# A four-layer hybrid decoder on one core: VectorE's running sums, modulated rows and rsqrt operands moved to PSUM, and the first layer's modulation computed two feature tiles at a time

## The chip, the cores and the metric

One core of one Trainium2 chip. The metric is device time in microseconds (us) of one execution of the whole program, the median of several runs.

## The reference

Four layers over 512 tokens of 1024 features, batch 1, all in float32. Layer i has mixer i mod 3: 0 is multi-head latent attention (MLA, 8 heads), 1 is sliding-window attention with sinks (SWA, 16 heads, window 128), 2 is native sparse attention (NSA). So layers 0 and 3 are MLA.

```python
cond = jax.nn.silu(c)
for i in range(DEPTH):
    shift, scale, gate = jnp.split(cond @ ada_w[i] + ada_b[i], 3, axis=-1)
    h = rmsnorm(x, norm_g[i]) * (1 + scale[:, None, :]) + shift[:, None, :]
    ...                      # x = x + gate * Mixer(h); mixer = (attention * silu(gate path)) @ w_out
# MLA: q_a, kv_a, k_pe, gate = split(h @ w_in, 256 | 128 | 64 | 1024)
#      q = rmsnorm(q_a) @ w_q_b ; kv = rmsnorm(kv_a) @ w_kv_b ; rope on k_pe and part of q
```

`ada_w[i]` is 1024 x 3072, so the modulation of a layer reads 12.6 MB. A third of it (shift, scale or gate) is 1024 x 1024.

## The kernel before, in words

Every float32 product on TensorE (PE) is made of three products of rounded parts: `mm3` issues hi*hi, hi*lo and lo*hi (lines 70, 71, 72). A weight piece of 512 columns comes by DMA from SyncE's queue (SP), ScalarE (ACT) rounds it to `wh` (line 103) and GpSimd (POOL) subtracts to get `wl` (line 104). VectorE (DVE) does the same subtraction for activations (line 66), evicts PSUM, and forms the softmax and the rotations.

The order of instructions on each engine is written by a planner at compile time: it takes the program's order as priority, and simulates when buffers come free. On the chip each engine then runs its list strictly in order.

**Modulation of layers 1 to 3 and the gate of layer 0.** `ada_steps` works on one third at a time: 16 loads of 128 x 512 of `ada_w` into three buffers; for each, VectorE multiplies by a column of `cond` and adds into `ada_acc`, a tile in SBUF (lines 315 and 317). For the thirds queued with a third argument True ((0, 2), (1, 0) and (3, 2)) the later half of the rows is multiplied by ScalarE (line 311) and added by GpSimd (line 313). At the end TensorE sums over the partitions (`rows` at line 323 or `cols` at line 329). There are ten such thirds. `queue_mods` puts the steps into a queue, and `mod_steps` takes them out at fixed places of the attention heads and of the output projection.

**First layer.** `start` loads the four token tiles of x (SP), squares them on ScalarE, makes the reciprocal root on VectorE (`rsqrt`, lines 78 to 83) and scales x on VectorE (line 1162). Then for each feature tile k of 8, `prep(k)` loads 1 MB of `ada_w` (two loads of 512 KB in runs of 128 floats), sums it over the 8 rows in `facc` (SBUF, lines 1179 and 1181; for k = 0 on TensorE, line 1186), sums over the partitions (line 1189), adds the bias (line 277), transposes x (line 151), modulates (line 1197) and splits into `hTh`, `hTl`. The products of tile k (four tiles of 448 columns and a gate tile of 512, 15 matmuls) follow. `angles()`, the rotation's sine and cosine, is called at k = 6.

**Norm of the later layers.** `norm_tile` transposes a normalised token tile into two PSUM banks of pool `tpp`. In each half ScalarE modulates two of the four feature tiles and VectorE two (lines 384, 386), into `hf` in SBUF; then the split (lines 387, 388).

**MLA's low-rank part.** The four token tiles of 448 columns are copied to `lat` in SBUF (lines 611, 613), squared on ScalarE, `rsqrt` runs on 128 x 8 tiles in SBUF (lines 85 to 87), `lat` is scaled (lines 625, 626) and transposed (line 151), and only then come the head projections. The rotation of the key part reads `lat` (lines 158, 161).

**PSUM.** Eight banks: projections `mmp`, transposes `tpp`, scores `sp`, outputs `op`: 2, 2, 2, 2 in layer 0 and 2, 3, 2, 1 in layers 1 to 3. Every softmax block is transposed through a `tpp` bank and split from there by ScalarE (line 65) and VectorE (line 66). The gate tiles of MLA take a bank of `op`.

## Time and profile before

| what | value |
|---|---|
| median of 3 runs | 1137.04 us (1131.63 to 1139.35) |
| span of the profiled execution | 1138.5 us |
| TensorE matmul busy | 1041.8 us, 92% of the span |
| VectorE / GpSimd / ScalarE busy | 836.5 / 651.8 / 634.3 us |
| HBM read and written | 124.17 MB and 8.39 MB |

The profiled execution has no time of its own beside its span; the span lies within the three runs, 1.5 us above their median, so what lies around the span is no more than the runs differ among themselves. An engine's busy time is time in which one of its instructions runs or is held, so a VectorE instruction that waits for something in the middle of its execution counts as busy and merely looks long. "Granted clock" is TensorE's: 1.00 is 2.4 GHz, 0.5 is 1.2 GHz, and a stretch between them is a mixture.

### The profile page before, as it was taken

The page shows a single profiled execution, that of the slowest core. Times are in us where ns is not written, and L with a number is a line of the kernel's source. Part 1 is how long each engine was busy: PE and PEld are TensorE (multiplying, and loading weights), DVE is VectorE, ACT ScalarE, POOL GpSimd, SP SyncE. Part 2 cuts the span into 40 slices and gives each one's busy share as a digit, 9 for nine tenths or more (in the row PEclk, how much of TensorE's full clock was granted, in tenths as well). Part 3 has the DMA queues.
Part 4 walks back from the last instruction along what each step waited for, and adds up shares of the span by engine and source line. Part 5 has one row for each costly group of instructions (what it writes and reads, how often), then busy time and mean ns, then how long its engine had stood idle before and what let it go on. Part 6 is the DMA issues. An engine that isn't in the chain of part 4 may idle for free.

```text
span 1138.5 us, 21101 instructions
## 1 busy us (share of the span) xinstructions
PE 1041.8 (92%) x6836; PEld 939.1 (82%) x6836; DVE 836.5 (73%) x2361; ACT 634.3 (56%) x1622; POOL 651.8 (57%) x781
## 2 busy tenths in 40 slices
PE   5798999989998998999899999999998896999997
PEld 4586888889887887999878798988888895889897
DVE  6967576588899787783748887789996687657435
ACT  3455666444545686356344567768784265656542
POOL 2564755292766784914665756757565627534473
PEclk9889999998989998999999899999999898999999
DMA  9935442374573212743662611211006526211141
GB/s 291 239 85 152 135 132 79 112 242 151 151 229 93 74 39 94 230 147 84 187 171 73 169 27 32 56 38 38 10 30 221 178 102 199 61 55 49 39 139 74
DMA packets 146026, 133.93 MB, mean 118 GB/s; under 512 B 31462, under 2 KB 118652, under 8 KB 145916
## 3 DMA queue, kind: packets, MB, share of 16 engines
q1 hardware_dynamic: 142688, 122.55, 37.0%
q10 hardware_dynamic: 3228, 10.04, 2.5%
q8 instruction: 54, 0.88, 0.3%
q14 instruction: 56, 0.46, 0.1%
HBM read 124.17 MB, written 8.39 MB: 116 GB/s over the span
## 4 chain that ended last, share of the span: by engine, by line
PE 60%; DVE 17%; DMA 8%; issue 6%; ACT 5%; POOL 4%; SPq 1%; DVEq 0%; ACTq 0%; POOLq 0%
PE mm L70 8%; PE mm L71 8%; PE mm L72 8%; PE tp L151 7%; DMA ada_w<-ada_w 6%; DVE ada_acc L317 4%; PE o L70 4%; PE o L71 3%; PE o L72 3%; DVE facc L1181 2%; PE mm L416 2%; PE s L966 1%; PE s L965 1%; PE o L974 1%; PE o L975 1%
## 5 line engine op out<-in xcount | busy, mean ns | idle before, releaser
L104 POOL TENSOR_TENSOR wl<-raw,wh 128x512 fp32r<-128x512 f32 (+2 forms) x206 | 274.9, 1346 | 127.7 <-ACT wh L103 103.6
L103 ACT ACTIVATE wh<-raw 128x512 fp32r<-128x512 f32 (+2 forms) x206 | 124.5, 612 | 113.8 <-PE o L71 27.8
L70 PE MATMUL mm<-wh,hTh 128*128 128x256 f32 (+2 forms) x512 | 153.7, 301 | 7.9 <-DVE sg L428 3.4
L71 PE MATMUL mm<-wl,hTh 128*128 128x256 f32 (+2 forms) x512 | 152.7, 298 | 0.0
L72 PE MATMUL mm<-wh,hTl 128*128 128x256 f32 (+2 forms) x512 | 152.4, 298 | 0.2 <-DVE hTl L388 0.2
L530 ACT ACTIVATE p<-p,negm 128x128 f32<-128x128 f32 (+3 forms) x192 | 107.0, 558 | 46.6 <-DVE negm L526 43.6
L70 PEld LDWEIGHTS mm<-wh,hTh 128*128 128x128 f32 x512 | 100.4, 196 | 10.9 <-DVE sg L428 3.9
L533 POOL TENSOR_SCALAR p<-p,rsum,bg 128x128 f32<-128x128 f32 (+3 forms) x128 | 82.0, 647 | 45.4 <-DVE rsum L532 36.3
L526 DVE CUSTOM_DVE_ANT_0 p<-s,mask 128x128 f32<-128x128 f32 (+3 forms) x192 | 91.0, 483 | 22.0 <-PE s L966 9.0
L71 PEld LDWEIGHTS mm<-wl,hTh 128*128 128x128 f32 x512 | 100.5, 196 | 1.6
L72 PEld LDWEIGHTS mm<-wh,hTl 128*128 128x128 f32 x512 | 100.4, 196 | 1.6 <-DVE hTl L388 0.4
L151 PE MATMUL tp<-ident,p 128*128 128x128 f32 x480 | 79.4, 274 | 1.9 <-POOL p L533 0.9
L533 POOL TENSOR_SCALAR p<-p,rsum 128x128 f32<-128x128 f32 (+1 forms) x64 | 34.7, 546 | 78.2 <-DVE rsum L532 71.2
L66 DVE TENSOR_TENSOR ptl<-tp,pth 128x512 fp32r<-128x512 f32 x108 | 72.2, 683 | 9.7 <-ACT pth L65 9.0
L481 POOL TENSOR_TENSOR x<-x,res 128x256 f32<-128x256 f32 x48 | 42.4, 888 | 60.8 <-DVE res L480 40.3
L65 ACT ACTIVATE pth<-tp 128x512 fp32r<-128x512 f32 x108 | 60.9, 591 | 26.1 <-PE tp L151 22.9
L151 PEld LDWEIGHTS tp<-ident,p 128*128 128x128 f32 x480 | 58.0, 140 | 12.2 <-POOL p L533 1.9
L355 ACT ACTIVATE sq_junk<-x 128x256 f32<-128x256 f32 x64 | 26.5, 414 | 67.5 <-POOL x L481 57.6
L317 DVE SCALAR_TENSOR_TENSOR ada_acc<-ada_w,res,ada_acc 128x512 f32<-128x512 f32 x42 | 52.3, 1265 | 11.0 <-DMA ada_w<-ada_w 10.7
L70 PE MATMUL mm<-wh,ogh 128*128 128x256 f32 x192 | 55.1, 288 | 3.3 <-DVE res L480 1.7
L72 PE MATMUL mm<-wh,ogl 128*128 128x256 f32 x192 | 53.9, 285 | 1.0 <-DVE ogl L66 0.8
L71 PE MATMUL mm<-wl,ogh 128*128 128x256 f32 x192 | 54.1, 282 | 0.0
(380 smaller groups left out, 3556.6 us busy)
## 6 DMA issues: line engine op xcount, KB each, us to landing
ada_w<-ada_w SPq DMA_DIRECT2D x160, 256.0 KB, 3.2
raw<-swa_w_in SPq DMA_DIRECT2D x36, 256.0 KB, 3.3
raw<-nsa_w_in SPq DMA_DIRECT2D x36, 256.0 KB, 3.1
aw<-ada_w SPq DMA_DIRECT2D x16, 512.0 KB, 7.1
raw<-mla_w_in SPq DMA_DIRECT2D x32, 256.0 KB, 3.1
raw<-mla_w_out SPq DMA_DIRECT2D x32, 256.0 KB, 2.8
xd<-x SPq DMA_DIRECT2D x12, 512.0 KB, 3.2
x<-xd ACTq DMA_DIRECT2D x12, 512.0 KB, 6.6
```

The lines of the kernel that those rows point to most:

```text
L65: self.nc.scalar.activation(hi, src, AF.Copy)
L66: self.nc.vector.tensor_sub(lo, src, hi.bitcast(F32))
L70: mm(out, ah, bh, start=start, stop=False, skip_group_check=True)
L71: mm(out, ah, bl, start=False, stop=False, skip_group_check=True)
L72: mm(out, al, bh, start=False, stop=stop, skip_group_check=True)
L103: nc.scalar.activation(wh, raw, AF.Copy)
L104: nc.gpsimd.tensor_sub(wl, raw, wh.bitcast(F32))
L151: self.nc.tensor.transpose(out, in_, self.ident[:k, :k])
L317: nc.vector.scalar_tensor_tensor(a, w, self.condl[:, k:k + 1], a, op0=OP.mult, op1=OP.add)
L526: nc.vector.tensor_tensor_reduce(p[:, :L], s, mask, -scale, init, op0=OP.add, op1=OP.min, accum_out=nm)
L530: nc.scalar.activation(p[:, :W], p[:, :W], AF.Exp, bias=nm, scale=-1.0, accum_out=sm)
L533: nc.gpsimd.tensor_scalar(p[:, :L], p[:, :L], r, 0.5 if gate is None else gate, op0=OP.mult, op1=OP.mult)
```

## The change

Six edits in one.

1. **Sums in PSUM.** Pool `accp` with one PSUM bank exists in layers 0, 1 and 3. `ada_steps` sums one half of 512 columns at a time in that bank (during the output projection, in a bank of `sp`), and the last of the eight adds writes SBUF. In NSA (layer 2) there is no such bank and the sum stays in SBUF. The ScalarE and GpSimd share of three thirds goes: every add is VectorE's. In the queue the closing step of a third now comes ahead of the next third's loads.
2. **Banks.** 2, 2, 2, 1, 1 in layers 0, 1 and 3: one output bank fewer in layer 0, one transpose bank fewer in layers 1 and 3. NSA keeps 2, 3, 2, 1.
3. **Modulated rows in PSUM.** `norm_tile` modulates in place in the transposes' bank, the first half all on ScalarE, the second half all on VectorE, and splits from there.
4. **MLA.** `rsqrt` has its input and its scratch in PSUM. The key part is rotated straight from the projection's bank, in the loop that copies the low-rank part.
5. **First layer.** Four groups of two feature tiles: eight loads of 256 KB in runs of 256 floats into twelve buffers, sums of 128 x 512 in PSUM, all on VectorE; no modulation on TensorE. x's reciprocal root has its six small steps on GpSimd, and x is scaled on ScalarE. The sine and cosine come before the sums. One of the four 448-column products takes a transpose bank.
6. `rsqrt` of one column uses `tensor_scalar` with two pointer scalars in place of `scalar_tensor_tensor`.

```diff
-BANKS = ((2, 3, 2, 1), (2, 3, 2, 1), (2, 3, 2, 1))
+BANKS = ((2, 2, 2, 1, 1), (2, 2, 2, 1, 1), (2, 3, 2, 1, 0))
-    def rsqrt(self, half, n, y):
+    def rsqrt(self, half, n, y, t=None, eng=None):
+        if n == 1:
+            t = self.small.tile([P, n], F32, name="rs_t", tag="rs_t")
+        eng = eng or nc.vector
         nc.vector.tensor_scalar(y.bitcast(I32), half.bitcast(I32), -0.5, 1593268703.0 - 2.0 ** 31, op0=OP.mult, op1=OP.add)
-        t = self.small.tile([P, n], F32, name="rs_t", tag=f"rs_t{n}")
         for _ in range(3):
             if n == 1:
-                nc.vector.scalar_tensor_tensor(t, y, half, y, op0=OP.mult, op1=OP.mult)
-                nc.vector.tensor_scalar(y, t, -1.5, y, op0=OP.add, op1=OP.mult)
+                eng.tensor_scalar(t, y, half, y, op0=OP.mult, op1=OP.mult)
+                eng.tensor_scalar(y, t, -1.5, y, op0=OP.add, op1=OP.mult)
             else:
-                nc.vector.tensor_mul(t, y, y)
-                nc.vector.tensor_mul(t, t, half)
+                nc.vector.tensor_mul(t, half, y)
+                nc.vector.tensor_mul(t, t, y)
...
+    def acc_bank(self):
+        if self.in_proj_out:
+            return self.sp.tile([P, 512], F32, name="s")
+        return self.accp and self.accp.tile([P, 512], F32, name="acc")
...
-                n = 4 if self.acc_bufs > 1 else 0
-                self.mods += loads[:n] + late + loads[n:]
+                self.mods += late + loads
...
-                for c in range(0, D, 512):
-                    a = acc[0][:, c:c + 512]
+                c = 512 * (step // 4)
+                if step % 4 == 0:
+                    acc[1:] = [self.acc_bank() or acc[0][:, c:c + 512]]
+                for k in (2 * (step % 4), 2 * (step % 4) + 1):
                     w = self.adaw.tile([P, 512], F32, name="ada_w", tag="ada_w", bufs=3)
                     nc.sync.dma_start(w, dr(A["ada_w"], l * D * 3 * D + k * 3 * D + third * D + c, [[KT * 3 * D, P], [1, 512]]))
-                    if pool and k > 3:
-                        d = w if k else a
-                        nc.scalar.activation(d, w, AF.Copy, scale=self.condl[:, k:k + 1])
-                        if k:
-                            nc.gpsimd.tensor_add(a, a, w)
-                    elif k == 0:
-                        nc.vector.tensor_scalar(a, w, self.condl[:, 0:1], None, op0=OP.mult)
+                    if k == 0:
+                        nc.vector.tensor_scalar(acc[1], w, self.condl[:, 0:1], None, op0=OP.mult)
                     else:
-                        nc.vector.scalar_tensor_tensor(a, w, self.condl[:, k:k + 1], a, op0=OP.mult, op1=OP.add)
+                        d = acc[0][:, c:c + 512] if k == KT - 1 else acc[1]
+                        nc.vector.scalar_tensor_tensor(d, w, self.condl[:, k:k + 1], acc[1], op0=OP.mult, op1=OP.add)
...
-                if kk in ACT_K:
-                    nc.scalar.activation(hf[:, kk, :], ps[:, k * P:(k + 1) * P], AF.Identity, scale=s, bias=b)
+                h = ps[:, k * P:(k + 1) * P]
+                if half == 0:
+                    nc.scalar.activation(h, h, AF.Identity, scale=s, bias=b)
                 else:
-                    nc.vector.tensor_scalar(hf[:, kk, :], ps[:, k * P:(k + 1) * P], s, b, op0=OP.mult, op1=OP.add)
-            nc.scalar.activation(self.nhTh[:, ks, t], hf[:, ks], AF.Copy)
-            nc.vector.tensor_sub(self.nhTl[:, ks, t], hf[:, ks], self.nhTh[:, ks, t].bitcast(F32))
+                    nc.vector.tensor_scalar(h, h, s, b, op0=OP.mult, op1=OP.add)
+            hf = ps.rearrange("p (k q) -> p k q", q=P)
+            self.split_dve(self.nhTh[:, ks, t], self.nhTl[:, ks, t], hf)
...                                                      # mla: low-rank part
+                k1 = ap.tile([P, 1, 2, 64], F32, name="kpe", tag="kpe", bufs=4)
+                self.rope_twice(ps[:, None, 384:448], 1, i, k1)
...
+            ps = self.sp.tile([P, 512], F32, name="s")
+            nc.vector.tensor_scalar(ps[:, 0:4], ss[:, 0:4], 0.5 / 256, 0.5 * EPS, op0=OP.mult, op1=OP.add)
+            nc.vector.tensor_scalar(ps[:, 4:8], ss[:, 4:8], 0.5 / 128, 0.5 * EPS, op0=OP.mult, op1=OP.add)
-            self.rsqrt(ss, 8, rs)
+            self.rsqrt(ps[:, 0:8], 8, rs, ps[:, 8:16])
...                                                      # start
+            for i, x in enumerate(xs):
+                nc.scalar.activation(junk, x, AF.Square, accum_out=ss[:, i:i + 1])
+            self.angles(pf, fr)
+            for i, x in enumerate(xs):
+                h = ss[:, i:i + 1]
+                nc.vector.tensor_scalar(h, h, 0.5 / D, 0.5 * EPS, op0=OP.mult, op1=OP.add)
+                self.rsqrt(h, 1, rstds[i], eng=nc.gpsimd)
+            for i, x in enumerate(xs):
+                nc.scalar.activation(x, x, AF.Copy, scale=rstds[i])
+            ps4 = [p.tile([P, 512], F32, name=n) for p, n in ((self.sp, "s"), (self.sp, "s"), (self.op, "o"), (self.tpp, "tp"))]
...
+            def columns(g):
+                pool, name = ((self.mmp, "mm"), (self.accp, "acc"))[g % 2]
+                a = pool.tile([P, 512], F32, name=name).rearrange("p (t n) -> p t n", t=2)
+                acc = ap.tile([P, 2, 256], F32, name="facc", tag="facc", bufs=2)
+                for r in range(KT):
+                    w = ap.tile([P, 2, 256], F32, name="aw", tag="aw", bufs=12)
+                    nc.sync.dma_start(w, dr(A["ada_w"], r * 3 * D + g * 256, [[KT * 3 * D, P], [D, 2], [1, 256]]))
+                    if r == 0:
+                        nc.vector.tensor_scalar(a, w, self.cond[:, 0:1], None, op0=OP.mult)
+                    else:
+                        nc.vector.scalar_tensor_tensor(acc if r == KT - 1 else a, w, self.cond[:, r:r + 1], a, op0=OP.mult, op1=OP.add)
+                weights(2 * g)
+                weights(2 * g + 1)
+                return acc
...
+            acc = columns(0)
+            self.vector_columns(vs)
+            modulation(0, acc)
+            features(0)
+            for k in range(KT):
+                g = k // 2 + 1
+                if k % 2 == 0 and g < 4:
+                    acc = columns(g)
+                elif g < 4:
+                    modulation(g, acc)
+                if k + 1 < KT:
+                    features(k + 1)
+                products(k)
```

## Rows read from the trace of the kernel before

**Rows 1.** The page: busy time by engine, and the chain that ended last by engine.
```profile
PE 1041.8 (92%) x6836; PEld 939.1 (82%) x6836; DVE 836.5 (73%) x2361; ACT 634.3 (56%) x1622; POOL 651.8 (57%) x781
...
PE 60%; DVE 17%; DMA 8%; issue 6%; ACT 5%; POOL 4%; SPq 1%; DVEq 0%; ACTq 0%; POOLq 0%
```

**Rows 2.** By stretch: length, busy us (instructions) of each engine, clock, DMA share, GB/s.
```profile
23.00:73.00 50.00, 41.48 (x171) 33.80 (x169) 41.45 (x91) 19.93 (x34) 28.16 (x21) 0.83 0.73 190
...
222.00:264.00 42.00, 38.26 (x298) 37.77 (x297) 32.79 (x59) 16.19 (x44) 34.02 (x27) 0.92 0.83 272
...
294.00:352.00 58.00, 50.58 (x299) 44.61 (x298) 52.87 (x115) 26.88 (x68) 44.43 (x54) 0.94 0.73 217
...
860.00:906.00 46.00, 37.92 (x280) 36.09 (x279) 30.01 (x50) 16.51 (x44) 33.29 (x27) 0.93 0.74 236
...
932.00:958.00 26.00, 14.76 (x69) 12.94 (x68) 23.02 (x38) 10.40 (x24) 17.41 (x12) 0.81 0.70 206
```

**Rows 3.** Groups by form over the whole span: count, busy us, mean ns, idle before.
```profile
L104 POOL TENSOR_TENSOR wl<-raw,wh 128x512 fp32r<-128x512 f32 x180 | 245.0, 1370 | 89.8 <-ACT wh L103 65.8 <-issue 18.6 <-PE mm L71 2.9
...
L66 DVE TENSOR_TENSOR ptl<-tp,pth 128x512 fp32r<-128x512 f32 x108 | 72.2, 683 | 9.7 <-ACT pth L65 9.0
L65 ACT ACTIVATE pth<-tp 128x512 fp32r<-128x512 f32 x108 | 60.9, 591 | 26.1 <-PE tp L151 22.9 <-DVE ada_v L277 2.0 <-DVE ogl L66 0.3
...
L317 DVE SCALAR_TENSOR_TENSOR ada_acc<-ada_w,res,ada_acc 128x512 f32<-128x512 f32 x42 | 52.3, 1265 | 11.0 <-DMA ada_w<-ada_w 10.7
...
L1181 DVE SCALAR_TENSOR_TENSOR facc<-aw,cond,facc 128x256 f32<-128x256 f32 x49 | 36.3, 751 | 0.6
...
L313 POOL TENSOR_TENSOR ada_acc<-ada_acc,ada_w 128x512 f32<-128x512 f32 x24 | 30.8, 1291 | 8.1 <-DMA ada_w<-ada_w 5.9 <-ACT ada_w L311 1.5 <-DVE rs_t L86 0.7
L317 DVE SCALAR_TENSOR_TENSOR ada_acc<-ada_w,kr,ada_acc 128x512 f32<-128x512 f32 x28 | 30.5, 1098 | 4.4 <-DMA ada_w<-ada_w 4.2
...
L428 DVE SCALAR_TENSOR_TENSOR sg<-g_th,o 128x512 f32<-128x512 f32 x15 | 10.3, 685 | 35.0 <-ACT g_th L425 35.0
```

**Rows 4.** Timeline of VectorE: start, us, line, operation, count; the first layer's sums.
```profile
35.33 3.02 DVE L1181 SCALAR_TENSOR_TENSOR facc<-aw,cond,facc 128x256 f32<-128x256 f32 x2
...
38.42 0.47 DVE L1181 SCALAR_TENSOR_TENSOR facc<-aw,cond,facc 128x256 f32<-128x256 f32 x1
```

**Rows 5.** Chain that ended last, 925 to 965 us: start, us, what.
```profile
947.00 1.16 DVE rs_t L85
...
948.17 0.18 DVE rs_t L86
...
954.84 2.82 PE tp L151 x12
```

**Rows 6.** Timeline of the first layer, ScalarE's last square.
```profile
9.77 1.06 ACT L341 ACTIVATE sq_junk<-x 128x1024 f32<-128x1024 f32 x1 [0.23 <-DMA x<-x]
```

**Rows 7.** Timeline of the first layer: first product, last sums, products after them, last product.
```profile
23.09 0.72 PE L70 MATMUL s<-wh,hTh 128*128 128x448 f32 x1
...
60.13 2.82 DVE L1181 SCALAR_TENSOR_TENSOR facc<-aw,cond,facc 128x256 f32<-128x256 f32 x2
...
66.38 0.58 PE L70 MATMUL s<-wh,hTh 128*128 128x448 f32 x1
...
72.85 0.40 PE L72 MATMUL mm<-hTh,wl 128*128 128x512 f32 x1
```

**Rows 8.** DMA issues up to 70 us: count, KB each, median us to landing.
```profile
aw<-ada_w SPq DMA_DIRECT2D x16, 512.0 KB, 7.1
```

**Rows 9.** By stretch: the loads of x, then those of the first layer's modulation.
```profile
4.00:8.00 4.00, 0.45 (x1) 0.18 (x1) 0.96 (x5) 2.13 (x4) 0.00 (x0) 1.00 1.02 412
8.00:42.00 34.00, 25.97 (x110) 22.36 (x110) 29.30 (x86) 10.58 (x20) 12.89 (x10) 0.95 1.12 292
```

**Rows 10.** TensorE's waits, 932 to 958 us: in total, times, longest.
```profile
PE tp L151 <- DVE lat L625: 11.2, 1, 11.2
```

**Rows 11.** TensorE's waits, 97 to 222 us, where there are two transpose banks.
```profile
PE tp L151 <- DVE mptl L66: 0.2, 1, 0.2
```

More of the change, by code (lines that the diff above doesn't have):

```diff
@@ L223, in vectors, with vector_columns @@
         nc.scalar.dma_start(v2[20:22, :], dr(A["mla_kv_norm_g"], 0, [[P, 2], [1, P]]))
+        self.vec = cp.tile([P, 160], F32, name="vec")
+        return v1, v2
+    def vector_columns(self, vs):
+        nc, (v1, v2) = self.nc, vs
         ps = self.tpp.tile([P, 512], F32, name="tp")
@@ L333, in ada_steps @@
         return [load(k) for k in range(KT)], rows if third == 2 else cols
-    def mean_sq(self, x, n, pool):
-        nc = self.nc
-        junk = pool.tile([P, D], F32, name="sq_junk", tag="sq_junk", bufs=1)
-        ss = self.small.tile([P, 1], F32, name="ss", tag="ss")
-        nc.scalar.activation(junk[:, :n], x, AF.Square, accum_out=ss)
-        nc.vector.tensor_scalar(ss, ss, 0.5 / n, 0.5 * EPS, op0=OP.mult, op1=OP.add)
-        return ss
     def load_x(self, src, i, pool, eng=None):
@@ L604, in mla @@
             ss = ap.tile([P, 8], F32, name="mss")
-            lat = []
+            lat, kpe = [], []
             w = None if first else self.wchunk(w_in, MLA_IN, 0, 448)
@@ L1112, in run @@
         self.psum = None
-        self.banks(2, 2, 2, 2)
+        self.banks(2, 2, 2, 1, 1)
         self.new_sg()
@@ L1143, in banks @@
         self.psum = ExitStack()
-        self.mmp, self.tpp, self.sp, self.op = (
-            self.psum.enter_context(self.tc.tile_pool(name=name, bufs=k, space=PSUM, reuse_waits="tile"))
-            for name, k in zip(("mmp", "tpp", "sp", "op"), n))
+        self.mmp, self.tpp, self.sp, self.op, self.accp = (
+            k and self.psum.enter_context(self.tc.tile_pool(name=name, bufs=k, space=PSUM, reuse_waits="tile"))
+            for name, k in zip(("mmp", "tpp", "sp", "op", "accp"), n))
     def start(self):
@@ L1174, in prep @@
                                          [[MLA_IN, P], [P * MLA_IN, 4], [1, P]], [4, P])
-                mp = self.mmp.tile([P, 512], F32, name="mm")
-                on_pe = PE_ADA.get(k, 0)
-                if on_pe < 2:
-                    acc = ap.tile([P, 2, P], F32, name="facc", tag="facc", bufs=4)[:, on_pe:]
-                    nc.vector.tensor_scalar(acc, aw[:, 0, on_pe:], self.cond[:, 0:1], None, op0=OP.mult)
-                    for r in range(1, KT):
-                        nc.vector.scalar_tensor_tensor(acc, aw[:, r, on_pe:], self.cond[:, r:r + 1], acc,
-                                                       op0=OP.mult, op1=OP.add)
@@ L1183, in prep @@
-                for t in range(2):
-                    if t < on_pe:
-                        for r in range(KT):
-                            nc.tensor.matmul(mp[:, t:t + 1], aw[:, r, t], self.cond[:, r:r + 1], start=r == 0,
-                                             stop=r == KT - 1, skip_group_check=True)
-                    else:
-                        nc.tensor.matmul(mp[:, t:t + 1], acc[:, t - on_pe], self.ones[:, 0:1], start=True, stop=True,
-                                         skip_group_check=True)
+            def columns(g):
[8 more added lines that the diff above has]
+                    else:
+                        nc.vector.scalar_tensor_tensor(acc if r == KT - 1 else a, w, self.cond[:, r:r + 1], a,
+                                                       op0=OP.mult, op1=OP.add)
+                weights(2 * g)
+                weights(2 * g + 1)
+                return acc
@@ L1191, in prep, with modulation @@
+            def modulation(g, acc):
+                mp = self.mmp.tile([P, 512], F32, name="mm")
+                for t in range(2):
+                    for k in range(2):
+                        nc.tensor.matmul(mp[:, 2 * t + k:2 * t + k + 1], acc[:, t, k * P:(k + 1) * P], self.ones[:, 0:1],
+                                         start=True, stop=True, skip_group_check=True)
                 for t in range(2):
-                    self.ada_cols(0, t, k, mp[:, t:t + 1])
+                    self.ada_cols(0, t, g * 2, mp[:, 2 * t:2 * t + 2])
```

79 lines of the change are left out of this document (34 added, 45 removed).

## The prediction

> **What bounds the kernel now.** I read the page first: TensorE is busy 92% of the span and VectorE 73%, yet the chain that ended last runs through TensorE for 60% only, 17% through VectorE, 8% through DMA [rows 1]. So the time to win is the idle time of TensorE and the low clock around it, about 97 us of idle in all (1138.5 - 1041.8). The view by stretch says where it lies. From 23 to 73 us TensorE is idle 8.5 of 50 us at a mean clock of 0.83; 3.7 of 42 us and 8.1 of 46 us in the first and third output projection; 7.4 of 58 us where SWA begins; 11.2 of 26 us in the low-rank part of layer 3 [rows 2]. In all of them VectorE or GpSimd runs near full.
>
> Next the groups by form. The same `scalar_tensor_tensor` of 128x512 takes 1265 or 1098 ns on average when both its tensors are in SBUF, and 685 ns when one is in PSUM; the subtraction with a PSUM input takes 683 [rows 3]. The timeline shows that this is no slow arithmetic: one add of `facc` lasts 0.47 us and two of the same form, a little earlier, 3.02 [rows 4]. The long ones run while GpSimd has its subtraction of 1370 ns [rows 3]. Even a 128x8 operation of `rsqrt` lasts 1.16 us, with one of 0.18 behind it [rows 5]. So VectorE with two SBUF inputs is held until GpSimd's instruction ends, and it holds everything queued behind it.
>
> The Trainium skill says this as a rule ("SBUF — State Buffer", Who interferes with whom): a VectorE instruction with two SBUF inputs contends with a GpSimd instruction that reads SBUF, and one with at most one SBUF input doesn't. The rows agree for PSUM inputs; no row here has VectorE writing PSUM. By that rule every excess below goes.
>
> **The first layer.** Before, x has landed at 9.8 us [rows 6], the first product starts at 23.1, the last sum ends at 62.95, products 6 and 7 start 3.4 us later and end at 73.25 [rows 7]. After:
> - Loads. 16 loads of 512 KB of `ada_w` [rows 8], eight of 224 KB and two of 256 KB of weights, 10.75 MB. They now run at 292 GB/s in runs of 512 bytes; x, in runs of 4096 bytes and loads of the same 512 KB, came at 412 [rows 9]. Runs of 1024 bytes lie between; I take 340, an estimate: 31.6 us, so the last `ada_w` lands near 40 (weights 6 and 7 come behind it). Ends: 26.1 and 36.8 us of loading.
> - Sums. 4 groups of 8 operations by 0.69 us (the row with one PSUM input [rows 3]; no row writes PSUM, so 0.47 to 1.1 as ends) are 22 us within those 32, against 49 adds by 751 ns and seven openings before [rows 3]. VectorE is no longer late.
> - First product. The first two tiles' 2.1 MB take 6.2 us from 9.8; then last sum, partition sum, bias, modulation and split, the 3.4 us from last sum to product [rows 7]: 19.6. x must be ready too: the last square ends near 10.9 [rows 6], GpSimd's six one-column steps and ScalarE's scaling come behind it, with the sine and cosine possibly between. No row has those steps; I take 21, ends 19 and 26.
> - TensorE. Its work from 23 to 73 is 41.48 us at a clock of 0.83, 34.4 us at full clock [rows 2]: 21 + 34.4 = 55.4. The loads' side gives 40 + 3.4 + two tiles of 3.4 (6.87 us for tiles 6 and 7 [rows 7]) = 50, so TensorE sets the end. I take 56, ends 54 and 67.5 (start at 26, all 41.5 us at the old clock). Term: 56 - 73.3 = **-17 us** (-19 to -6).
> - Given back: the norm of the low-rank part follows, and gate tiles cover it. With one output bank each gate waits until ScalarE and VectorE have read the last (0.69 [rows 3] and about as much on ScalarE): twice 1.3, **+3** (0 to +6).
>
> **Layer 3's low-rank part.** TensorE waits 11.2 us for `lat` [rows 10], which VectorE delivers at 954.84; in front of it on VectorE stand five small operations held like the one of 1.16 us, which have 0.18 when free [rows 5], and sums of twice their length. In PSUM the five give 5 us, and the sums queued between them some 2: **-7** (-2 to -11, the whole idle time).
>
> **Sums elsewhere.** 14 adds in each of three output projections, 42 by 1265 ns, and 28 by 1098 in SWA [rows 3]: at 0.69 VectorE has 24 and 11 us less. Little of it is on the path: these stretches also wait for `ada_w` itself (10.7 and 4.2 us of VectorE's idle time [rows 3]), which still comes through three buffers. A VectorE add that waits for a load keeps rotations and evictions queued behind it, as before. The idle time of TensorE there bounds the gain. I take half of what is left of it: **-4** for the projections (0 to -9), **-3** for SWA (0 to -7). NSA keeps its sums in SBUF: 0. The 24 adds that leave GpSimd (31 us [rows 3]) and come to VectorE (16.6 us at 0.69) are in stretches where TensorE is busy: 0 (-2 to +3). SP's queue has the same loads in another order.
>
> A rule against the change: a PSUM operand caps a float32 VectorE operation at one element a cycle (the Trainium skill, "VectorE: DVE Perf Modes", Why PSUM operands drop a tier), so the opening product of each sum loses its double rate. No row shows that product in PSUM. At most half of 0.69 us is lost by it on each of 20, 7 us of VectorE's time over the span; that changes no term, since no such product is among the rows of a stall.
>
> **Modulated rows, one-column root.** The same eight modulations and two splits per tile, at PSUM prices, and one engine per bank; the in-place write holds the bank a little longer: 0 (-2 to +2).
>
> **One transpose bank fewer.** In layers 1 and 3 about 103 uses of a transpose bank (28 softmax blocks, 20 query and key tiles and 8 norm halves in SWA; 32 score tiles and 15 others in MLA). A bank is held for ScalarE's 591 ns, VectorE's 683 [rows 3] and the transposes. Layer 0 has two banks already, and there TensorE waits 0.2 us for that split [rows 11]. So I take **+4** (0 to +15).
>
> **The sum.** -17 + 3 - 7 - 4 - 3 + 4 = -24 us. 1138.5 - 24 = 1114.5 in a profile; the median lay 1.5 below the span, so **1114** for the median. A measurement of this kernel tells a change from none at about 1%, 11 us.
>
> **Rivals.**
> 1. *The first layer stays bound by its start and its loads.* ScalarE has 4 scalings and the sine and cosine to do in front of the first modulation, and GpSimd 24 dependent steps; loads at 292 GB/s. The term is -6 instead of -17: 1138.5 - 13 = 1125. For it: each engine runs its list in order, and with its stalls TensorE had a clock of 0.83 here [rows 2]. Against: TensorE has work for two tiles per group. The Trainium skill would have smaller loads be slower ("DMA: Bandwidth & Descriptors", Measured: 341 GB/s at 1 MB, 138 at 64 KB). Near 240 GB/s for 256 KB, an estimate from that page, the loading would take 45 us and the time be some 1124; the two kinds of load of one size [rows 9] speak against size as the cause.
> 2. *The held instructions were not the path.* Outside the first layer the wait for loads takes the place of the held adds: terms 4 and 3 vanish and layer 3 gives 3. 1138.5 - 13 = 1125. With rival 1 as well: 1136, no change.
> 3. *Slower: the transpose bank.* In SWA and layer 3, with two banks instead of three, a bank held for about 1.8 us comes round 0.3 us later at each use; if the queues of ScalarE and VectorE double the hold, 0.6: 103 x 0.6 = 62 us, against the other terms' -28: 1172. It decides from 0.27 us per use. For it: VectorE is 91% busy at SWA's start [rows 2]. Against: the 0.2 us that TensorE waits where there are two banks [rows 11].
> 4. *The change doesn't do what it says*: the planner, which knows nothing of held instructions, orders the queues so that adds wait in front of products. That is a part of 2.
>
> **Chances.** Forecast (1104 to 1124) 0.50; below it 0.06; rival 1 0.14; rival 2 0.11; both 0.08; rival 3 0.11. Rivals 1 and 2 lie on the 1% line, half to each side: faster 0.68, same 0.21, slower 0.11. The range 1098 to 1144 leaves out the best ends and most of rival 3.
>
> **What would show it.** Right: the adds to PSUM at 0.6 to 0.75 us without long ones; the first layer's last product near 56 us; `rsqrt` of 128x8 at 0.2 us an operation in layer 3, and TensorE's wait for `lat` there at 3 to 5 us; output projections and SWA's start shorter by 1 to 3 us each; TensorE's waits on transposes in SWA under 4 us. Wrong: first product after 26 us, or TensorE waiting on `ptl` and `mptl` for tens of us.

## The result: 1110.2 us after 1136.7, and the profile after

After takes 1110.2 us (median of 4 runs, 1104.4 to 1112.3) against 1136.7 of before on the same chip; the ratio is 0.9756, with a 95% interval of 0.9728 to 0.9783. Forecast were 1114 and a range of 1098 to 1144: the time and the sign were right. The sum was not made of the terms that the prediction gave it, as the stages below show.

The page of after, busy time by engine and the chain that ended last [rows 1]:

```profile
PE 1024.1 (92%) x6808; PEld 922.1 (83%) x6808; DVE 778.3 (70%) x2321; ACT 623.6 (56%) x1602; POOL 594.5 (54%) x781
...
PE 62%; DVE 13%; DMA 6%; issue 5%; ACT 4%; POOL 3%; SPq 0%; ACTq 0%; DVEq 0%; POOLq 0%
```

VectorE has 58 us less and GpSimd 57. For GpSimd that is more than the 31 us of adds that it lost. The groups by form say where the rest went (count, busy us, mean ns, idle before) [rows 3]:

```profile
L104 POOL TENSOR_TENSOR wl<-raw,wh 128x512 fp32r<-128x512 f32 x180 | 233.2, 1306 | 115.1 <-ACT wh L103 91.9 <-ACT xh L63 11.7 <-PE mm L70 5.8
...
L324 DVE SCALAR_TENSOR_TENSOR s<-ada_w,res,s 128x512 f32<-128x512 f32 x36 | 27.2, 754 | 21.0 <-DMA ada_w<-ada_w 20.7
L324 DVE SCALAR_TENSOR_TENSOR ada_acc<-ada_w,krn,ada_acc 128x512 f32<-128x512 f32 x28 | 27.0, 966 | 8.6 <-DMA ada_w<-ada_w 8.4
L324 DVE SCALAR_TENSOR_TENSOR acc<-ada_w,cond,acc 128x512 f32<-128x512 f32 x36 | 27.0, 750 | 9.0 <-DMA ada_w<-ada_w 8.6
```

The adds with a PSUM tile (`s`, `acc`) take 754 and 750 ns, those that stayed in SBUF in NSA 966. GpSimd's own subtraction has become shorter too, 1306 ns against 1370: each of the two had been holding the other (experiment 2 shows both directions). In return the adds in the output projections now wait for their loads, 20.7 us against 10.7.

The windows of the stretches that answer to rows 2 (length, then busy us of PE, PEld, DVE, ACT, POOL, then clock, DMA share, GB/s):

```profile
23.00:62.00 39.00, 33.00 (x164) 29.52 (x165) 19.02 (x34) 17.45 (x29) 27.04 (x23) 0.96 0.80 241
211.00:253.00 42.00, 42.00 (x362) 42.00 (x361) 29.57 (x77) 19.06 (x53) 28.81 (x28) 1.00 0.83 272
279.00:337.00 58.00, 55.35 (x355) 48.98 (x354) 46.06 (x137) 31.40 (x86) 39.75 (x68) 1.00 0.64 191
834.00:880.00 46.00, 41.36 (x300) 40.04 (x299) 23.22 (x57) 16.68 (x44) 26.98 (x27) 0.89 0.75 240
906.00:932.00 26.00, 20.31 (x93) 16.34 (x91) 19.67 (x46) 11.98 (x26) 16.12 (x14) 0.93 0.82 241
```

TensorE had been idle 3.7 us in the first output projection and 7.4 where SWA begins [rows 2]; now it is 0 and 2.7, at full clock. In the third output projection 4.6 of 46 us are idle, where it had been 8.1, and in layer 3's low-rank part 5.7 of 26, where it had been 11.2.

**The span by stages.** Each mark is one TensorE instruction or lat copy of the traces, so the columns add up to the spans. "b1" and "e2" are two of the experiments below: b1 is the kernel before with all adds on VectorE, e2 is after with all running sums behind the start in SBUF.

| stage, us | before | b1 | e2 | after |
|---|---|---|---|---|
| start, to the last copy of `lat` | 72.9 | 70.7 | 63.0 | 62.9 |
| to the first head's scores | 28.5 | 28.6 | 31.4 | 30.7 |
| MLA heads, to the first output projection | 96.7 | 99.3 | 103.3 | 98.5 |
| first output projection | 72.9 | 71.5 | 65.0 | 60.9 |
| to SWA's first scores | 23.2 | 23.2 | 26.2 | 26.1 |
| SWA | 144.5 | 142.7 | 140.5 | 133.4 |
| second output projection | 62.0 | 66.0 | 62.2 | 61.4 |
| to NSA's first scores | 103.1 | 100.9 | 103.7 | 109.3 |
| NSA | 246.0 | 243.4 | 241.7 | 241.3 |
| third output projection | 66.7 | 65.8 | 63.0 | 63.8 |
| to layer 3's first scores | 59.6 | 60.7 | 59.1 | 57.0 |
| the rest | 162.4 | 162.7 | 163.5 | 163.8 |
| span | 1138.5 | 1135.5 | 1122.6 | 1109.1 |

From before to after: start -10 (forecast -17), behind it +2.2 (+3), SWA -11 (-3), first output projection -12 (a part of -4), way to layer 3's scores -2.6 (-7), way to NSA's scores +6.2 (forecast 0).

The marks don't enclose the same work in every kernel, because the lists differ. The windows of the MLA heads and of the first output projection, before and then after (the number behind PE's busy time counts its instructions):

```profile
101.40:198.10 96.70, 90.78 (x539) 77.21 (x538) 66.10 (x187) 64.06 (x154) 56.44 (x59) 1.00 0.42 123
198.10:271.00 72.90, 67.18 (x521) 65.09 (x521) 53.14 (x123) 32.49 (x86) 40.26 (x38) 0.95 0.56 181
...
93.60:192.10 98.50, 95.19 (x569) 81.97 (x570) 77.51 (x218) 56.43 (x146) 39.57 (x49) 1.00 0.41 121
192.10:253.00 60.90, 58.88 (x488) 57.28 (x487) 41.12 (x107) 27.65 (x76) 31.22 (x32) 1.00 0.66 217
```

Some 30 instructions of the heads lie in front of the projection's mark in after and behind it before; in the same way some 30 lie in front of SWA's scores in after (223 against 198) and behind them before. In this b1 is like before (543 and 519) and e2 like after (571 and 489). So the four stages from the heads to the end of SWA are better taken together: before 337.3 us, b1 336.7, e2 335.0, after 318.9, with 21.0, 19.3, 19.9 and 9.8 us in which TensorE is idle.

**The start after.** ScalarE [rows 6 for before]:

```profile
8.24 1.28 ACT L267 ACT_TABLE_LOAD   x1
...
11.11 1.28 ACT L270 ACT_TABLE_LOAD   x1
...
14.59 1.04 ACT L1162 ACTIVATE sq_junk<-x 128x1024 f32<-128x1024 f32 x1
...
19.25 1.15 ACT L1169 ACTIVATE x<-x,rstd 128x1024 f32<-128x1024 f32 x1 [1.16 <-POOL rstd L83]
```

The sine and cosine, with two table loads of 1.28 us, lie between the squares. The last square starts at 14.59 instead of 9.77, and the last scaled tile of x starts at 19.25. TensorE's first and last product [rows 7]:

```profile
26.51 0.74 PE L68 MATMUL s<-wh,hTh 128*128 128x448 f32 x1 [3.88 <-ACT hTh L1215]
...
62.68 0.40 PE L70 MATMUL mm<-hTh,wl 128*128 128x512 f32 x1
```

Between them stands the first product of the fifth tile, behind an idle stretch:

```profile
46.14 0.66 PE L151 MATMUL tp<-ident,x 128*128 128x128 f32 x4 [1.92 <-ACT fhf L1213]
47.18 0.74 PE L68 MATMUL s<-wh,hTh 128*128 128x448 f32 x1 [0.38 <-ACT hTh L1215]
```

And VectorE: the bias of the second group of two tiles, the last add of the third group, the last add of the fourth and the bias that follows it:

```profile
34.10 0.23 DVE L281 TENSOR_TENSOR ada_v<-mm,vec 128x2 f32<-128x2 f32 x2 [3.90 <-PE mm L1203]
...
41.55 0.74 DVE L1193 SCALAR_TENSOR_TENSOR facc<-aw,cond,mm 128x512 f32<-128x512 f32 x1
...
46.14 0.75 DVE L1193 SCALAR_TENSOR_TENSOR facc<-aw,cond,acc 128x512 f32<-128x512 f32 x1 [0.20 <-DMA aw<-ada_w]
...
51.55 0.23 DVE L281 TENSOR_TENSOR ada_v<-mm,vec 128x2 f32<-128x2 f32 x2 [4.66 <-PE mm L1203]
```

So the first product came at 26.5 us (forecast 21), the last load was used at 46.1 (40) and the last product ended at 63.1 (56). VectorE's wait of 4.66 us for the fourth group's partition sum costs nothing, since TensorE works without a gap from 47.2 us to the end. What came late was the third group. VectorE waits 3.90 us for the second group's partition sum, which stands behind products in TensorE's list; then it adds the third group's rows in turn with the fourth's, without a wait for a load, until 42.3. By then TensorE is about to run out of products: it has four of the eight tiles left when it starts again at 47.2. The windows around it:

```profile
43.30:46.90 3.60, 1.58 (x13) 1.26 (x11) 2.88 (x7) 1.59 (x3) 1.23 (x2) 1.00 1.13 285
46.90:50.30 3.40, 3.12 (x8) 2.82 (x9) 0.00 (x0) 2.04 (x4) 3.40 (x3) 0.50 0.52 136
```

TensorE worked 1.6 of 3.6 us, and then its clock was granted at the lower level, 1.2 GHz, for the first products of these four tiles.

**Layer 3's low-rank part after**, VectorE's timeline [rows 5 for before]:

```profile
912.87 0.76 DVE L324 SCALAR_TENSOR_TENSOR acc<-ada_w,cond,acc 128x512 f32<-128x512 f32 x1 [1.26 <-DMA ada_w<-ada_w]
...
914.57 0.75 DVE L324 SCALAR_TENSOR_TENSOR ada_acc<-ada_w,cond,acc 128x512 f32<-128x512 f32 x1 [0.56 <-DMA ada_w<-ada_w]
...
915.63 0.17 DVE L85 TENSOR_TENSOR s<-s,mrs 128x8 f32<-128x8 f32 x1
...
919.39 0.76 DVE L324 SCALAR_TENSOR_TENSOR acc<-ada_w,cond,acc 128x512 f32<-128x512 f32 x1 [0.81 <-DMA ada_w<-ada_w]
...
921.13 1.35 DVE L628 TENSOR_SCALAR lat<-lat,mrs 128x256 f32<-128x256 f32 x1
...
923.61 0.34 DVE L628 TENSOR_SCALAR lat<-lat,mrs 128x256 f32<-128x256 f32 x1
```

The steps of the root take 0.17 us each, as forecast. But the sums in front of them and between them wait for their loads, up to 1.26 us each, and everything queued behind waits with them. From the last copy of `lat` (910.7) to the first transpose of it (927.3) it is 16.6 us; before it was 14.4 (940.4 to 954.8). TensorE's longest wait of 906 to 932 us stands in another place [rows 10]:

```profile
PE o L68 <- DVE sg L426: 4.8, 1, 4.8
```

That is a gate tile waiting for the one output bank, which VectorE's list gives back late.

### The profile page after: what moved, and what is told of

It is laid out like the page before. It is cut to its first block, busy times and chain, and to the rows that moved or that the text cites. A ratio compares the mean times of both kernels' runs of the same rounds, so it can differ in the third digit from the quotient of the medians.

```text
span 1109.1 us, 21056 instructions
## 1 busy us (share of the span) xinstructions
PE 1024.1 (92%) x6808; PEld 922.1 (83%) x6808; DVE 778.3 (70%) x2321; ACT 623.6 (56%) x1602; POOL 594.5 (54%) x781
## 4 chain that ended last, share of the span: by engine, by line
PE 62%; DVE 13%; DMA 6%; issue 5%; ACT 4%; POOL 3%; SPq 0%; ACTq 0%; DVEq 0%; POOLq 0%
PE mm L68 9%; PE mm L69 9%; PE mm L70 9%; PE tp L151 7%; DMA ada_w<-ada_w 5%; PE o L68 4%; PE o L69 4%; PE o L70 4%; PE mm L414 2%; PE s L964 1%; PE s L963 1%; PE o L972 1%; PE o L973 1%; DVE acc L324 1%; POOL wl L104 1%
## 5 line engine op out<-in xcount | busy, mean ns | idle before, releaser
L104 POOL TENSOR_TENSOR wl<-raw,wh 128x512 fp32r<-128x512 f32 (+2 forms) x206 | 258.9, 1269 | 145.4 <-ACT wh L103 119.0
L68 PEld LDWEIGHTS mm<-wh,hTh 128*128 128x128 f32 x512 | 98.5, 192 | 9.8 <-issue 5.8
L70 PEld LDWEIGHTS mm<-wh,hTl 128*128 128x128 f32 x512 | 98.5, 192 | 2.2 <-DVE hTl L64 0.7
L63 ACT ACTIVATE pth<-tp 128x512 fp32r<-128x512 f32 x108 | 61.4, 591 | 23.2 <-PE tp L151 19.9
L151 PEld LDWEIGHTS tp<-ident,p 128*128 128x128 f32 x480 | 58.4, 140 | 12.2 <-issue 2.9
L479 POOL TENSOR_TENSOR x<-x,res 128x256 f32<-128x256 f32 x48 | 36.5, 766 | 58.7 <-DVE res L478 38.1
L68 PE MATMUL o<-hTh,wh 128*128 128x512 f32 x120 | 49.3, 410 | 8.0 <-DVE sg L426 6.5
L563 ACT ACTIVATE qs<-tp 64x256 fp32r<-64x256 f32 x96 | 35.8, 376 | 31.4 <-DVE qs L564 17.7
```

Source lines behind the costliest of these rows:

```text
L63: self.nc.scalar.activation(hi, src, AF.Copy)
L68: mm(out, ah, bh, start=start, stop=False, skip_group_check=True)
L70: mm(out, al, bh, start=False, stop=stop, skip_group_check=True)
L104: nc.gpsimd.tensor_sub(wl, raw, wh.bitcast(F32))
L151: self.nc.tensor.transpose(out, in_, self.ident[:k, :k])
L479: (nc.vector if c == 3 else nc.gpsimd).tensor_add(xs[i][:, cs], xs[i][:, cs], t)
```

## The experiments

Each ratio is that of a kernel to the kernel before on the same chip, with its 95% interval; 0.01 is 11.4 us. One thing must be known to read them: the planner writes the order anew for every edit, and how much of it changes differs. By tile and shape TensorE's 6808 matmuls come in the same order in the fifth and the ninth experiment as in after; in the sixth 6773 of them keep their place in it, in the second 6356. And even where TensorE's order is the same (after and the fifth experiment), stages of the two traces differ by up to 2.5 us. Differences of a few us far from an edit are therefore no evidence about it.

**1. After with the old start** (the fourth product bank is then `accp`'s).

```diff
-            ps4 = [... ((self.sp, "s"), (self.sp, "s"), (self.op, "o"), (self.tpp, "tp"))]
+            # vectors(), angles() and start() of before
+            ps = [... ((self.sp, "s"), (self.sp, "s"), (self.op, "o"), (self.accp, "acc"))]
```

> Only the first layer's start is as in the kernel before (loads of one feature tile, sums in SBUF, tile 0's modulation on TensorE, x normalised on VectorE, sine and cosine late); everything else is as after. The prediction's term (-17 us for the start, 3 given back) says 1110 + 14 = 1124 us. The stage marks of the two traces say less: the start's products ended 10 us earlier and by the first head's scores 8 were left, so 1118. If the start's end is hidden by what follows: 1110.

1114.5 us, ratio 0.9817 (0.9776 to 0.9857): 4 us above after by the medians, 7 by the ratios. In the stages the start ends 9.1 us later and the first head's scores come 9.1 later, and at the end 8.5 are left. The first layer is worth 4 to 9 us, not 14.

**2. All running sums in SBUF.**

```diff
     def acc_bank(self):
-        if self.in_proj_out:
-            return self.sp.tile([P, 512], F32, name="s")
-        return self.accp and self.accp.tile([P, 512], F32, name="acc")
+        return None
```

> All running sums behind the start go back to SBUF, the banks stay as after (the fifth one idle). The prediction gave the sums elsewhere 7 us (output projections 4, sliding-window layer 3) and some 2 of layer 3's part: 1119 us. The stage marks of the two traces (first output projection 12 us shorter, sliding-window layer 11 shorter) say 1130 or more. If the held adds were not on the path: 1110. In the trace the adds should be long again, 1.0 to 1.3 us on average against 0.75.

1126.3 us, ratio 0.9915 (0.9888 to 0.9942): the sums in PSUM are worth 16 us by the medians and 18 by the ratios, the largest part of the whole. The groups of this run, the sums of the output projections and of MLA:

```profile
L322 DVE SCALAR_TENSOR_TENSOR ada_acc<-ada_w,res,ada_acc 128x512 f32<-128x512 f32 x42 | 53.6, 1276 | 13.5 <-DMA ada_w<-ada_w 12.8
L322 DVE SCALAR_TENSOR_TENSOR ada_acc<-ada_w,cond,ada_acc 128x512 f32<-128x512 f32 x42 | 36.8, 878 | 5.2 <-DMA ada_w<-ada_w 5.0
```

The same adds as 754 and 750 ns above. The shortest of them take 0.73 us in SBUF as in PSUM; only the long ones are gone.

Set against GpSimd's instructions, the adds show what held them. Of the 140 adds of this run with both tensors in SBUF, 49 begin while no GpSimd instruction runs, and none of these takes over 0.75 us. The other 91 begin within one: 78 of them take longer than 0.8 us, and 76 of the 78 end 0.5 to 0.7 us after the GpSimd instruction ends. In after, 96 of the 140 adds with a PSUM tensor (those of the start with them) begin within a GpSimd instruction, and none takes over 0.76 us. The hold goes the other way as well: in this run the 44 subtractions of 128x512 that begin within such an SBUF add take 1.70 us on average, the other 168 take 1.30. In the first output projection, this run and then after:

```profile
L104 POOL TENSOR_TENSOR wl<-raw,wh 128x512 fp32r<-128x512 f32 x8 | 12.8, 1619 | 0.0
...
L104 POOL TENSOR_TENSOR wl<-raw,wh 128x512 fp32r<-128x512 f32 x8 | 10.3, 1309 | 0.8 <-ACT wh L103 0.8
```

By the table of stages, e2 against after, the gain lies in the MLA heads of layer 0 (4.8), the first output projection (4.1) and SWA (7.1), whose marks enclose nearly the same work in these two kernels; 5.6 us are lost again on the way to NSA's scores, and no run shows why.

**3. Sums in PSUM in the output projections alone.**

```diff
-        return self.accp and self.accp.tile([P, 512], F32, name="acc")
+        return None
```

> Running sums in PSUM in the output projections alone; in the attention parts they are in SBUF. The prediction: sliding-window layer 3 and layer 3's part 2, so 1115 us. By the stage marks: sliding-window layer 11, so 1121 or more. If the projections carry all of the sums' gain: 1110.

1120.4 us, ratio 0.9856 (0.9812 to 0.9899). So the attention parts hold 10 to 11 us of the sums' gain and the projections 6 to 7. SWA takes 138.4 us here, 5 more than after.

**4. The same with three transpose banks in layers 1 and 3.**

```diff
-BANKS = ((2, 2, 2, 1, 1), (2, 2, 2, 1, 1), (2, 3, 2, 1, 0))
+BANKS = ((2, 3, 2, 1, 0), (2, 3, 2, 1, 0), (2, 3, 2, 1, 0))
```

> As the run with sums in PSUM in the output projections alone, but the bank that is idle there is given back to the transposes in layers 1 and 3 (three banks again). The difference of the two is the price of one transpose bank fewer: the prediction says 4 us (0 to 15) less than that run, rival 3 says 28 to 62 less, and if two banks are enough there is no difference.

1117.7 us, ratio 0.9836 (0.9794 to 0.9879): 2 to 3 us below the run before, within both intervals. Rival 3's 28 to 62 us are ruled out for these layers; the forecast's 4 can't be told from nothing. SWA itself was longer with the third bank in this plan (146.2 us against 138.4).

**5. Sine and cosine late.**

```diff
-            self.angles(pf, fr)                       # behind the squares
+                if k == 6:
+                    self.angles(pf, fr)
```

> After, with the sine and cosine back at the seventh feature tile, behind the normalisation of x on ScalarE and VectorE. If the sine and cosine in front of the normalisation made the first product late (26.5 us where the prediction had 21), it starts at 22 to 23. If TensorE's work then sets the end, as the prediction has it, the last product of the start comes 3 to 4 us earlier and the time is 1106 us; if the loads of the modulation set it (rival 1), the end of the start stays within 1 us and the time at 1110.

1104.2 us, ratio 0.9745 (0.9705 to 0.9785). The edit didn't do what it was for: the planner put the sine in front of the squares all the same (table load at 7.96 us), and the first product started at 26.2. The start ended within 0.5 us of after's, TensorE's order is that of after, and by the ratios the two kernels are equal. Nothing follows about the start from it.

**6. Layer 3's last sums behind the scaling of `lat`.**

```diff
+            if not first:
+                self.condl = self.small.tile([P, KT], F32, name="cond3", tag="cond3", bufs=1)
+                nc.vector.scalar_tensor_tensor(self.condl, lat[3][:, 376:384], 0.0, self.cond, op0=OP.mult, op1=OP.add)
```

> After, with the sums of layer 3's gate third made to begin behind the scaling of lat (their factors, cond, come from a copy that reads the scaled lat; the value is cond). The theory from the trace of after: VectorE's queue had sums in front of the steps of the root that waited for their loads, so lat's transposes began 16.6 us behind the last copy. Without them: 8 to 11 us, and 1110 - 6 = 1104 us. Rival: the sums that come later wait in front of the first heads' rotations and evictions, and the gain is given back: 1108 to 1110 with the early transposes all the same.

1110.2 us, ratio 0.9788 (0.9755 to 0.9822): no gain. VectorE's timeline of this run:

```profile
908.45 0.17 DVE L85 TENSOR_TENSOR s<-s,mrs 128x8 f32<-128x8 f32 x1
...
910.10 0.17 DVE L87 SCALAR_TENSOR_TENSOR mrs<-s,mrs 128x8 f32<-128x8 f32 x1
910.30 0.35 DVE L628 TENSOR_SCALAR lat<-lat,mrs 128x256 f32<-128x256 f32 x1
...
922.47 1.55 DVE L324 SCALAR_TENSOR_TENSOR acc<-ada_w,cond,acc 128x512 f32<-128x512 f32 x2 [2.15 <-DMA ada_w<-ada_w]
```

The nine steps of the root now run in 2 us without a gap, and the first transpose of `lat` comes 6.0 us behind the last copy instead of 16.6. So the sums, with their waits for loads, were what stood in front of it. But from the last copy to the first head's scores it is 36.9 us, where after has 34.6: the sums wait for the same loads later (2.15 us in front of the rotations), and TensorE waits 2.7 us for `rope_b` there. The gain was given back within the stage; the rival was right.

**7. The root in SBUF.**

```diff
-            self.rsqrt(ps[:, 0:8], 8, rs, ps[:, 8:16])
+            self.rsqrt(ss, 8, rs, ap.tile([P, 8], F32, name="mrt"))
```

> After, with the root of 128x8 in SBUF again (input and scratch), nothing else. The prediction: five small operations held by about 1 us each, so layer 3's part is 5 us longer: 1115 us. Rival: the loads of the sums queued between them set the pace, and the held operations fill time that was waited anyway: 1110 to 1111.

1111.1 us, ratio 0.9799 (0.9764 to 0.9835). The whole run can't tell 1 us from 5, the stage can: last copy to first transpose 16.6 us, as after, and 34.5 to the first scores (34.6). In SBUF one step of the nine took 0.71 us, the others 0.15 to 0.22. The root's move to PSUM is worth nothing here.

**8. All sums in SBUF, with a share for ScalarE and GpSimd** in the three thirds that had it before. It is not quite the order of before: a sum goes half by half here.

```diff
+                    if pool and k > 3:
+                        nc.scalar.activation(w, w, AF.Copy, scale=self.condl[:, k:k + 1])
+                        nc.gpsimd.tensor_add(acc[1], acc[1], w)
```

> The run with all sums in SBUF (1126 us), and in two of the ten thirds' places where the kernel before did it ((0, 2), (1, 0) and (3, 2)) the later half of the rows is again scaled by ScalarE and added by GpSimd. The prediction put no time on the move of these adds (0, -2 to +3): 1126. The remainder between that run and the kernel before, some 4 to 5 us that the first layer does not explain, would put it here: 1130 to 1132, with the first output projection longer again.

1136.4 us, ratio 1.0018 (0.9997 to 1.0039), 10 us above the second experiment. But the first output projection stayed at 65.4 us. Layer 3 alone became longer: 42.1 us from the last copy of `lat` to the first scores instead of 37.0. The tenth experiment shows that this is not the price of the share in the kernel before.

**9. Sine and cosine tied to the modulation**, by a term of zero times it.

```diff
+        nc.vector.scalar_tensor_tensor(pf, self.mod[0, 0][:, 2:2 + NT], 0.0, pf, op0=OP.mult, op1=OP.add)
```

> The same aim as the run with the angles late, where ScalarE still had the sine in front of its squares: now the positions take a term of zero times the modulation of tiles 2 to 5, so that the sine and cosine can't begin before about 43 us. If they made the first product late, it starts at 22 to 24 us (26.5 after, 26.2 with the angles late). If the loads set the end of the start, its last product stays at 61 to 63 us all the same, and the time at 1104 to 1110; if TensorE's work sets it, the last product comes at 58 to 59 and the time 3 to 4 us below.

1105.9 us, ratio 0.9745 (0.9697 to 0.9793), by the ratios the same as after. TensorE's first and last product:

```profile
23.99 0.74 PE L68 MATMUL s<-wh,hTh 128*128 128x448 f32 x1 [3.88 <-ACT hTh L1215]
...
61.93 0.40 PE L70 MATMUL mm<-hTh,wl 128*128 128x512 f32 x1
```

The first came 2.5 us earlier, the last 0.75. So the sine and cosine did delay the first product, and it hardly matters, but the loads aren't shown to be the reason. VectorE's bias of the second group and last add of the third:

```profile
32.43 0.23 DVE L282 TENSOR_TENSOR ada_v<-mm,vec 128x2 f32<-128x2 f32 x2 [3.66 <-PE mm L1203]
...
39.92 0.74 DVE L1193 SCALAR_TENSOR_TENSOR facc<-aw,cond,mm 128x512 f32<-128x512 f32 x1
```

The wait for TensorE's partition sum is there again. The third group's sum ends 1.6 us earlier than in after, its first product comes at 46.4 instead of 47.2, and the last four tiles take the same 15.9 us.

**10. The kernel before without the share.**

```diff
-                    if pool and k > 3:
+                    if False:
```

> The kernel before with one edit: in the three thirds where ScalarE and GpSimd had the later half of the rows, VectorE now does all adds, in SBUF as before. The prediction put no time on this move: 1137 us (1134 to 1140). The run with all sums in SBUF against the one with the share put 10 us on it: 1127.

1140.1 us, ratio 1.0041 (1.0018 to 1.0064). The move of the 24 adds to VectorE costs 5 us while sums are in SBUF; it brings nothing. My theory from experiment 8 has fallen.

**11. NSA with the banks of the other layers.**

```diff
-BANKS = ((2, 2, 2, 1, 1), (2, 2, 2, 1, 1), (2, 3, 2, 1, 0))
+BANKS = ((2, 2, 2, 1, 1), (2, 2, 2, 1, 1), (2, 2, 2, 1, 1))
```

> After, with the banks of NSA as in the other layers (one transpose bank fewer, one bank for sums), so that its 30 adds go to PSUM as well. Sums that took 16 us with 84 adds in three layers would give 3 to 6 here: 1105 us. Rival 3 in NSA: the third transpose bank is worth more there, 1112 to 1120. By the prediction's own sizes (24 adds on the path for little): 1108 to 1111.

1130.5 us, ratio 0.9955 (0.9935 to 0.9976): 20 us above after. Its sums in NSA do take 752 ns. The NSA heads take 256.7 us instead of 241.3, the third output projection 68.4 instead of 63.8. The split behind the softmax transposes, first after's row over the whole span, then this run's (the three numbers behind the bar are busy us, mean ns and idle before):

```profile
L64 DVE TENSOR_TENSOR ptl<-tp,pth 128x512 fp32r<-128x512 f32 x108 | 72.4, 684 | 6.9 <-ACT pth L63 6.2
```

```profile
L64 DVE TENSOR_TENSOR ptl<-tp,pth 128x512 fp32r<-128x512 f32 x108 | 73.2, 686 | 16.1 <-ACT pth L63 15.3
```

VectorE waits 9 us longer for ScalarE's half of the split, while the split is no slower. TensorE's idle time in the NSA heads is 11.3 us instead of 5.6, and 4.8 us of it are waits for split tiles (1.0 in after). That fits rival 3: 15.4 us over the some 90 four-block and compressed splits of NSA would be 0.17 us per use. But the run takes a bank and moves the sums in one edit, and where the rest of the 15.4 us lies isn't shown. In the layers where the change took the bank nothing like it was found (experiment 4).

**12. Two side edits of the change in the kernel before**, on top of experiment 10: the tile of the sum in a pool that is never closed, and the closing step first.

```diff
-                acc.append(self.adaw.tile([P, D], F32, name="ada_acc", tag="ada_acc", bufs=self.acc_bufs))
+                acc.append(self.adap.tile([P, D], F32, name="ada_acc", tag="ada_acc", bufs=1))
-                self.mods += loads[:n] + late + loads[n:]
+                self.mods += late + loads
```

> The kernel before with all adds on VectorE (1140 us) and two side edits of the change that the prediction passed over: the tile of the sum lies in a pool that lives through the whole program (one buffer), and the closing step of a third comes ahead of the next third's loads. Sums stay in SBUF, three transpose banks, old start. In the kernel before, SP's first load of ada_w in the first output projection waits 17 to 20 us, in all kernels with the change 13. If these two edits carry that, the first output projection shrinks from 71.5 us to 65 and the time is 1133; if the modulated rows and the root do, both stay: 1139 to 1141 and 71 us.

1143.5 us, ratio 1.0068 (1.0042 to 1.0095). The first output projection takes 70.1 us; SP's wait is 16.5. These two edits are not the reason why it is 6.5 us shorter in e2 than in b1. The reason is the marks: e2 has some 30 of the stage's instructions in the stage before, and over the four stages together it is 1.7 us shorter, less than a single stage can differ between two traces.

No kernel of the twelve is faster than after by more than the intervals allow.

## Why the prediction was right, and where it wasn't

The total is right by luck: the first layer was over-sized by about as much as the sums elsewhere were under-sized. By the ratios, sums 18 and first layer 7 make 25 of 27.7 us; the remaining 3 lie within the intervals. Of the signs that it named, the adds (0.75 us), the steps of the root (0.17) and the transposes' waits in SWA came true; the last product of the start came at 63.1 us, not near 56, and the first one after 26 us, which it had called a sign of being wrong.

- **What held VectorE.** Right, and the root of the gain: adds to PSUM lost the long ones, and the long ones in SBUF end with GpSimd's instruction (experiment 2). Its size, 0.69 us, was 0.75. The section of the Trainium skill named there ("SBUF — State Buffer", Who interferes with whom) makes an exception that the prediction left out: an instruction with one SBUF input can contend too when it is a double-rate `tensor_scalar`. A row here agrees: the scaling of `lat`, with one tensor in SBUF, takes 0.34 us, and 1.35 at 921.13 us, where GpSimd's subtractions run from 921.04 to 923.60.
- **First layer, -17.** The step that failed is the loads' side, "40 + 3.4 + two tiles". The rate was right (349 GB/s from 8 to 46 us, 340 taken), but the last load was used at 46.1 us, not 40: SP's queue held other loads between them, 512 KB of the gate's bias at 25.3 us among them, so 13.3 MB came in these 38 us where 10.75 were counted. And four tiles were left then, not two, because the third group's sum had ended only at 42.3 us, behind a wait of VectorE for a partition sum that TensorE's list has late. These tiles took 15.9 us, the first 3.4 of them at half the clock. That this wait, and not the loads, set the end is read from the traces of after and experiment 9; no run changes it alone. The first product came 5.5 us late. By the term's own sum (first product and 34.4 us of TensorE's work) that alone makes 60.9 us; but in experiment 9, where the sum makes 58.4, the last product ended at 62.3, so 2.5 us of the delay cost under 1 us. The term measured -10 in the traces and 4 to 9 in experiment 1. Rival 1 was right that the start stays bound, and its -6 lies within that; its loads at 292 GB/s are not what was seen. The estimate of 240 GB/s beside it, from the page's table (the Trainium skill, "DMA: Bandwidth & Descriptors", Measured), fits less: the 256 KB loads and those between them moved 349 GB/s. Two small sums of this part are off: 9.8 + 6.2 + 3.4 is 19.4, not 19.6, and loads of 45 us give 1121 by the prediction's own terms, not 1124; nothing hangs on either.
- **Cover lost by one output bank, +3.** Right in size: +2.2 us between the start and the first scores. TensorE waits 2.9 us there for the one output bank, 0.2 before; no run has the second bank back.
- **Layer 3's low-rank part, -7.** Wrong in its mechanism. "The five give 5 us" failed: with the root back in SBUF the stage is no longer (experiment 7). The sums between the steps wait for loads, and without them the rest of the stage takes the time (experiment 6). With these sums in SBUF the first transpose even comes earlier, 12.5 us behind the last copy in experiment 2 and 11.1 in experiment 3, where after has 16.6; their lists differ from after's. What is late next was the question to ask. This is rival 2, in this stage alone.
- **Output projections -4 and SWA -3.** The mechanism was right, the size too small: 6 to 7 us for the projections, 10 to 11 for the attention parts, of which SWA has 5 to 7 and layer 0's heads 5. The prediction bounded the gain by TensorE's idle time in the stretches that it looked at, and it looked at no stretch of layer 0's heads. Nor is idle time the whole bound: over the four stages after is 16.1 us shorter than e2 with 10.1 us less of it, and the heads and the projection run at full clock where e2 has 0.98 and 0.97.
- **24 adds moved, 0.** In SBUF they cost 5 us (experiment 10). What they cost in PSUM was not measured, since GpSimd has no part in a PSUM sum here.
- **One transpose bank, +4.** Not told from 0 in layers 1 and 3 (experiment 4), and right to be small there; TensorE's waits on transposes in SWA are 0.7 us in after, where under 4 was forecast. In NSA the same exchange of banks costs 20 us, which fits rival 3's mechanism (experiment 11).
- **Norm rows, 0.** Not tried by themselves, nor was the one-column root. The first output projection is 6.5 us shorter in e2 than in b1 and the way to SWA's scores 3 us longer, but that is work on the other side of the marks. Over the four stages the two differ by 1.7 us, so these edits and the banks together are worth little there.
- **The rule on PSUM operands' rate.** As that rule has it, the opening product takes 0.75 us in PSUM and 0.46 to 0.48 in SBUF when undisturbed, so 0.27 us is lost on each. On average it took 0.71 to 0.98 in SBUF in experiment 2, so nothing is lost in the sum.

## What to carry to other kernels

When an engine's instruction looks long, find its shortest copy and see who runs during the long ones; moving one operand out of SBUF can then gain on both engines, and more than the idle time of the stretches in view. Where an engine runs its list in order, a saved microsecond counts only if the next thing in the list is ready, so ask for each stall what is late next: here it was a partition sum in the start and the loads in layer 3. A bank is priced by the layer that uses it: one transpose bank fewer cost too little to measure in SWA and 20 us of the whole in NSA, together with the sums' move there.

## What the runs showed of the hardware that was not expected

- GpSimd's subtraction of 128x512 is shortened by VectorE's move as well: in the first output projection 1604 ns before, 1309 after, and 1619 with the sums back in SBUF (experiment 2). The hold goes both ways.
- One-column steps on GpSimd take 346 and 267 ns at the start, VectorE's one-column steps 151; 24 of GpSimd's stood in front of the last scaling of x.
- Loads of 256 KB in runs of 1024 bytes, with the weights between them, moved 349 GB/s together, against 292 for 512 KB in runs of 512 bytes [rows 9]: the run's length, not the load's size, went with the rate.
